# Splitting four weight tiles of the second layer during the first layer's FFN

## The chip, the cores and the metric

The kernel runs on one core of a Trainium2 chip. The metric is the device time of one execution in microseconds (us). A chip has several engines with a queue each: TensorE (PE) multiplies, VectorE (DVE), ScalarE (ACT) and GpSimd (POOL) work element by element, and SyncE (SP) issues the transfers from memory. Each engine takes its instructions strictly in the order of its own list.

## The reference

A two-layer decoder trunk on 512 tokens of width 1024. What matters here is the seam between layer 0's feed-forward part and layer 1's attention:

```
x = x + (jax.nn.silu(g) * u) @ ffn_w_down[i]            # end of layer 0
h = rmsnorm(x, attn_norm[1])
cols = split_cols(h @ nsa_w_in[0], NSA_COLS)             # q, kc, vc, ks, vs, kw, vw, gates
k_cmp = gelu(blocks(kc + pos) @ ck_w1) @ ck_w2           # compression of keys
v_cmp = gelu(blocks(vc + pos) @ cv_w1) @ cv_w2           # compression of values
o = g0 * attend(q, k_cmp, v_cmp) + g1 * attend(rope(q), rope(ks), vs) + g2 * attend(rope(q), rope(kw), vw)
```

Layer 1 has 12 query heads in 6 pairs and three branches of attention: over compressed blocks, over selected blocks (keys `ks`), and over a window (keys `kw`).

## The kernel before, in words

**Products in two parts.** Every weight tile is 128 x 1024 and is multiplied in a split form: `hi` is the tile rounded to a shorter float, `lo` is what is missing, and a product is three matmuls, hi x hi, hi x lo of the activations, and lo x hi (lines 177, 178 and 179 of `mm3`). A projection of one 128-column tile is 8 x 3 = 24 matmuls of 512 columns.

**Splitting a weight.** `weight` (line 159) takes the next place of three rings, loads the raw tile (SP, line 163), makes `hi` by a cast (ACT at line 150 or DVE at line 148) and `lo` by a subtraction (DVE at line 165, or POOL, which goes through `Pieces` at line 83 in pieces of 256 columns, four to a tile). Which engine does it is read from the strings of `PLAN`, one after the other. The rings have 4 raw places, 3 for `hi` and 3 for `lo`, so that a tile can be split only when PE has finished the tile three before it.

**The FFN.** `ffn` (line 594) goes through two halves of 11 blocks. For each block two tiles (`g` and `u`, 22 loads `in_wf` in a half) are multiplied with x, then ACT, POOL and DVE make silu(g) * u (lines 606 to 609) and split it (lines 611 and 612); the 11 split blocks are `acts`. After that, 8 output tiles are made from `acts` with two weight tiles each (`in_wd`, 768 and 640 columns). In the second half of layer 0 each output tile also gives the next layer's input `xh`, `xl` and a square for the norm.

**The start of layer 1.** `nsa` (line 897) runs the words of `SEQ[1]`: `vc ks kc q:0 v ck kw h:0 plan:5 cv q:1 c:0 ...`. `vc`, `kc`, `ks`, `kw` and `q:j` are projections of one tile. `v` is `values` (line 970), 96 matmuls of 292 columns into four banks of PSUM, which ACT and DVE then empty (lines 989, 990, 991). `ck` and `cv` are `compress` (line 862) for keys and values: `cy` tiles are made by DVE (line 874), cast by ACT (875) and split by POOL; then come 16 steps of two matmuls, of 128 and 64 columns (lines 880, 881), half of them with the weight tile `cw1[which, 0]` and half with `cw1[which, 1]`; a gelu (lines 883 to 893) and one more product (line 944) follow. `h`, `w` and `c` are a head's scores in the three branches (lines 380 and 381, 385, 391, 409 to 411), capital letters the products with the values behind them (transposes at line 418, copies at 426 and 427, products at 441).

**What sets the order.** The words are only the order in which the program is written. The build gives every instruction a place in its engine's list by a model of its own, so that the four lists interleave several words, and a small change moves instructions further down too.

**The tag `xg`.** `BUFS` has 8 places of 128 x 1024 under the tag `xg`. Before the change only the end of layer 1 uses them (`last_gain`, line 633, and `down_last`, line 639).

Of the kernel before, what the change touches and what calls it, by code (L numbers as in the profile page):

```python
# [11 lines left out]
F32R = mybir.dt.float32r  # L12
# [6 lines left out]
P = 128  # L19
S = 512  # L20
# [9 lines left out]
OUT = -3e38  # L30
DOWN_SPLIT = (6, 5)
HALVED = 2
LAST = ("PPVP", "VVVV")
BUFS = {"xs": 17, "p": 10, "u": 8, "q": 12, "z": 2, "q1": 8, "qi": 4, "cy": 2, "k": 8, "m": 6, "r": 3, "t": 6, "o": 26, "o2": 6, "xg": 8}
RINGS = {"wr": 4, "wh": 3, "wl": 3}
# [29 lines left out]
W1 = ["kc", "vc", "ks", "kw"] + [f"q{j}" for j in range(6)] + ["qm0", "qm1"]  # L65


def r32(ap):
    return ap.bitcast(F32)
# [25 lines left out]
class Trunk:  # L95
# [498 lines left out]
    def ffn(self, i):  # L594
        nc, io = self.nc, self.io
        xs, row = self.xs, None
        for half in range(2):
            acts = []
            for e in range(NFF // 2):
                j = half * (NFF // 2) + e  # L600
                g = self.proj(io["wf"][i, 2 * j], xs)
                u = self.proj(io["wf"][i, 2 * j + 1], xs, "S")
                if row is None:
                    row = self.stats()[1]
                a = self.slot("t", "fa")
                nc.vector.tensor_mul(a, g, row)  # L606
                nc.scalar.activation(a, a, AF.Silu)  # L607
                self.pool.tensor_mul(a, a, row)
                nc.vector.tensor_mul(a, a, u)  # L609
                hi, lo = self.pair("o", "f")  # L610
                nc.scalar.copy(hi, a)
                nc.vector.tensor_sub(lo, a, r32(hi))
                acts.append((hi, lo))
            for d in range(KC):
                if i and half and d == KC - HALVED:
                    self.down_last(acts)
                    break
                ps = self.ps("mm")
                k = 0
                for m in DOWN_SPLIT:  # L620
                    w = self.weight(io["wd"][i, half, d, :, k * P : (k + m) * P], m * P)
                    for e in range(m):
                        sl = slice(e * P, (e + 1) * P)
                        self.mm3(ps, (w[0][:, sl], w[1][:, sl]), acts[k], k == 0, k == NFF // 2 - 1)
                        k += 1
                nc.vector.tensor_add(self.x[d], self.x[d], ps)  # L626
                if half:
                    self.absorb(d, 1 if i == 0 else None)
                    if i:
                        self.last_gain(d, slice(0, S))  # L630


    def last_gain(self, c, sl):
# [5 lines left out]
    def down_last(self, acts):  # L639

        nc, cs, ws = self.nc, range(KC - HALVED, KC), []
        for c in cs:
# [14 lines left out]
        for h in range(2):  # L657
# [11 lines left out]
            flat = self.slot("r", "row")[:, :NM]  # L669
            for m in sorted(range(KC // 2), key=lambda m: LAST[h][m], reverse=True):  # L670
                o = self.slot("p", "out").rearrange("p (e t) -> p e t", e=2)
                wide = lambda t: t[:, None, :].to_broadcast([P, 2, NM])
                if LAST[h][m] == "V":
                    nc.vector.tensor_mul(o, self.xg[m][:, :, sl], wide(row))
                else:
                    if LAST[h].index("P") == m:
                        nc.scalar.copy(flat, row)
# [184 lines left out]
    def compress(self, z, which):  # L862

        nc, io = self.nc, self.io
        pos = self.small(16, "pos", bufs=2)
        nc.sync.dma_start(pos, io["pos"][which])
        ps = self.ps("mm")[:, :P]
        split = lambda t: t.rearrange("p (g c j) -> p g c j", g=2, j=8)
        for u in range(2):
            full = self.slot("t", "cy")  # L870
            both = self.slot("cy", "cy", F32R, 2 * S).rearrange("p (a n) -> p a n", a=2)
            nc.gpsimd.memset(split(full)[:, :, 31], 0.0)
            for g in range(2):
                nc.vector.tensor_add(split(full)[:, g, :31], split(z)[:, g, u : u + 31], pos[:, None, 8 * u : 8 * u + 8].to_broadcast([P, 31, 8]))
            nc.scalar.copy(both[:, 0], full)
            self.pool.tensor_sub(both[:, 1], full, r32(both[:, 0]))
            hi, lo = self.weight(io["cw1"][which, u], 8 * P)
            for j in range(8):
                js = slice(j * P, (j + 1) * P)
                nc.tensor.matmul(ps, hi[:, js], both[:, :, j::8], start=u + j == 0, stop=False)  # L880
                nc.tensor.matmul(ps[:, :64], lo[:, js], both[:, 0, j::8], start=False, stop=u == 1 and j == 7)
        hid = self.small(64, "gh", bufs=2)
        nc.scalar.copy(hid, ps[:, :64])
        nc.vector.tensor_add(hid, hid, ps[:, 64:])
        t = self.small(64, "gt", bufs=2)
        o = self.small(128, "go", bufs=1)
        nc.scalar.activation(t, hid, AF.Square)
        nc.vector.tensor_scalar(t, t, 0.044715, 1.0, op0=ALU.mult, op1=ALU.add)
        nc.vector.tensor_mul(t, t, hid)
        nc.scalar.activation(t, t, AF.Tanh, scale=float(np.sqrt(2 / np.pi)))  # L890
        ov = o.rearrange("p (g e c) -> p g e c", g=2, e=2)
        for e in range(2):
            nc.vector.scalar_tensor_tensor(ov[:, :, e], t.rearrange("p (g c) -> p g c", g=2), 1.0, hid.rearrange("p (g c) -> p g c", g=2),
                                           op0=ALU.add, op1=ALU.mult)
        return ov

    def nsa(self):
        nc, io = self.nc, self.io
        xs = self.xs
        w = {n: io["w1"][t] for t, n in enumerate(W1)}  # L900
        lay = self.lay
        self.cmask, self.cm01 = (lay[:, n * P : (n + 1) * P].rearrange("p (b c) -> p b c", b=NB) for n in range(2))
        cw2, self.gates = lay[:, 2 * P : 2 * P + 192], lay[:, 2 * P + 192 :].rearrange("p (b h) -> p b h", b=NB)
        for t, n in ((self.cmask, "cmask"), (self.cm01, "cm01"), (cw2, "cw2")):
            nc.sync.dma_start(t, io[n])

        col, row = self.stats()
        self.plan(4)
        self.o, self.ready, q = {}, {"row"}, {}
        self.turn = self.flip = False  # L910

        def query(j):
            ps = self.proj(w[f"q{j}"], xs)
            self.o[j] = self.parts(self.rowed(ps, row), self.pair("o", "o"))
            q[2 * j], q[2 * j + 1] = self.stacks(self.rope(ps, tabs), "q1")

        mkv, z, keys = [], {}, {}
        tabs = self.tables(row)

        def key(n):  # L920
            keys[n == "kw"] = self.twins(self.rope(self.proj(w[n], xs), tabs))

        def unfold(n):
            z[n] = self.unfold(self.proj(w[n], xs), row)

        def comp_keys():
            self.comp_keys(self.compress(z["kc"], 0), cw2)

        def comp_values():
            self.comp_values(self.compress(z["vc"], 1), cw2)  # L930

        heads = [self.nsa_units(h, q, keys) for h in range(NH)]
        does = {"q": query, "mq": lambda j: self.mem_query(j, w, xs, row), "ks": lambda: key("ks"), "kw": lambda: key("kw"), "kc": lambda: unfold("kc"),
                "vc": lambda: unfold("vc"), "ck": comp_keys, "cv": comp_values, "v": lambda: self.values(col, xs),
                "mkv": lambda: mkv.extend(self.mem_kv(1)), "o": lambda n: self.out_part(1, n % KC, CHUNKS[1][n // KC], "mm"), "plan": self.plan}
        units = {"c": self.comp_unit, "h": lambda h: heads[h][0], "w": lambda h: heads[h][1],
                 "m": lambda j: self.mem_unit(j, mkv)}
        self.pipeline(SEQ[1], units, does)
        self.add_out(1)
# [228 lines left out]
```

## Time and profile before

| what | value |
|---|---|
| time, median of 3 runs | 1274.98 us (1273.6 to 1275.56) |
| time of the profiled execution | 1277.64 us |
| its span, first to last instruction | 1275.9 us |
| PE busy | 1234.9 us, 97% |
| DVE / ACT / POOL busy | 622.1 / 545.7 / 798.4 us |
| mean granted clock of PE | 0.98 |

The profiled execution took 2.66 us more than the median of the runs. A row of the profile gives a start or a window in us from the first instruction. Busy PE time is modelled from overlapping matmuls, so that a busy PE may still be slow; the granted clock (1.00 is 2.4 GHz, 0.50 is 1.2 GHz) stands beside it. In square brackets at the end of an instruction's row stands how long its engine had idled before it, and which instruction ended that.

### The profile page before, as it was taken

To read this page: it belongs to the slowest core of one execution; us is meant where nothing else is said; L and a number is where in the kernel's file an instruction comes from. 1 tells how busy PE (TensorE), PEld (TensorE's weight loads), DVE (VectorE), ACT (ScalarE), POOL (GpSimd) and SP (SyncE) were. 2 spreads that over 40 slices of the span, in tenths; PEclk is the share of its full clock that TensorE was granted. 3 is DMA by queue.
4 is the path that set the end of the run, shared out by engine and by line. 5 is a ranking of instruction groups with operands and counts; after the bars stand their busy time and mean duration, and the time that the engine had idled before them with its cause. 6 is when DMAs were issued, how large, how long until landed. Compare 5 with 4: busy or idle time off the path is not lost.

```text
span 1275.9 us, 17100 instructions
## 1 busy us (share of the span) xinstructions
PE 1234.9 (97%) x5882; PEld 1026.0 (80%) x5882; DVE 622.1 (49%) x1379; ACT 545.7 (43%) x1059; POOL 798.4 (63%) x1124
## 2 busy tenths in 40 slices
PE   7999889999999999999999999999999999999996
PEld 5888558888888888888888788887888888888886
DVE  6799976632221222234678998896521210111113
ACT  5535896433321223332247776785333322322231
POOL 9988884865543455447277674355986645667573
PEclk9999999999999999999986999999999999999998
DMA  7222002333223333223321101103232234333231
GB/s 267 89 74 89 11 1 76 99 99 99 89 78 100 118 95 99 81 89 116 107 99 50 36 15 57 32 32 118 78 96 96 85 88 114 111 97 91 69 91 66
DMA packets 40262, 108.44 MB, mean 85 GB/s; under 512 B 4720, under 2 KB 10480, under 8 KB 40176
## 3 DMA queue, kind: packets, MB, share of 16 engines
q1 hardware_dynamic: 40176, 107.36, 27.2%
q8 instruction: 46, 0.75, 0.3%
q14 instruction: 40, 0.33, 0.1%
HBM read 105.25 MB, written 2.10 MB: 84 GB/s over the span
## 4 chain that ended last, share of the span: by engine, by line
PE 77%; DVE 14%; ACT 3%; POOL 2%; DMA 2%; issue 1%; SPq 0%; DVEq 0%; ACTq 0%; POOLq 0%
PE ps L179 23%; PE ps L178 23%; PE ps L177 23%; PE ps L441 3%; PE ps L418 2%; DVE sc L690 2%; DVE stay L689 2%; DVE p L385 1%; DVE ul L427 1%; DMA mem<-in_memT 1%; POOL sq L83 1%; PE ps L380 1%; ACT p L391 1%; PE ps L381 1%; POOL stay L83 1%
## 5 line engine op out<-in xcount | busy, mean ns | idle before, releaser
L83 POOL TENSOR_TENSOR stay<-stay,stay 128x256 fp32r<-128x256 f32 (+1 forms) x601 | 441.5, 764 | 306.7 <-ACT stay L150 166.0
L150 ACT CAST stay<-stay 128x1024 fp32r<-128x1024 f32 (+4 forms) x208 | 189.4, 911 | 518.6 <-PE ps L178 455.3
L177 PE MATMUL ps<-xh,stay 128*128 128x512 f32 x912 | 358.9, 394 | 6.8 <-ACT xh L238 6.5
L179 PE MATMUL ps<-xh,stay 128*128 128x512 f32 x912 | 359.1, 394 | 1.2 <-DVE stay L165 1.2
L178 PE MATMUL ps<-xl,stay 128*128 128x512 f32 x912 | 358.0, 393 | 0.5 <-DVE xl L239 0.5
L177 PEld LDWEIGHTS ps<-xh,stay 128*128 128x128 f32 x912 | 173.4, 190 | 43.1 <-ACT xh L238 6.5
L179 PEld LDWEIGHTS ps<-xh,stay 128*128 128x128 f32 x912 | 173.0, 190 | 37.6 <-DVE stay L165 1.5
L178 PEld LDWEIGHTS ps<-xl,stay 128*128 128x128 f32 x912 | 172.9, 190 | 37.0 <-DVE xl L239 1.0
L178 PE MATMUL ps<-fl,stay 128*128 128x512 f32 (+1 forms) x352 | 134.8, 383 | 0.0
L179 PE MATMUL ps<-fh,stay 128*128 128x512 f32 (+1 forms) x352 | 134.6, 382 | 0.0
L177 PE MATMUL ps<-fh,stay 128*128 128x512 f32 (+1 forms) x352 | 134.6, 382 | 0.0
L609 DVE TENSOR_TENSOR fa<-fa,ps 128x512 f32<-128x512 f32 x44 | 30.2, 687 | 183.5 <-PE ps L179 166.1
L626 DVE TENSOR_TENSOR stay<-stay,ps 128x512 f32<-128x512 f32 x30 | 20.7, 689 | 155.6 <-PE ps L179 155.6
L606 DVE TENSOR_TENSOR fa<-ps,row 128x512 f32<-128x512 f32 x44 | 30.2, 690 | 128.2 <-PE ps L179 116.5
L391 ACT ACTIVATE p<-p,stay 128x384 f32<-128x384 f32 (+3 forms) x144 | 80.2, 559 | 18.0 <-DVE stay L385 17.4
L83 POOL TENSOR_TENSOR fa<-fa,row 128x256 f32<-128x256 f32 x88 | 65.3, 764 | 24.9 <-ACT fa L607 24.9
L177 PEld LDWEIGHTS ps<-fh,stay 128*128 128x128 f32 x352 | 66.1, 188 | 12.9
L178 PEld LDWEIGHTS ps<-fl,stay 128*128 128x128 f32 x352 | 66.1, 188 | 12.9
L179 PEld LDWEIGHTS ps<-fh,stay 128*128 128x128 f32 x352 | 66.2, 188 | 12.8
L83 POOL TENSOR_TENSOR p<-p,stay 128x128 f32<-128x128 f32 (+1 forms) x106 | 56.1, 557 | 32.4 <-DVE stay L401 21.7
L427 DVE TENSOR_TENSOR ul<-ps,uh 128x512 fp32r<-128x512 f32 (+1 forms) x103 | 62.7, 619 | 7.1 <-ACT uh L426 5.3
L418 PE MATMUL ps<-stay,p 128*128 128x128 f32 x360 | 55.8, 278 | 5.1 <-POOL p L83 2.1
(273 smaller groups left out, 2018.2 us busy)
## 6 DMA issues: line engine op xcount, KB each, us to landing
stay<-in_wf SPq DMA_DIRECT2D x88, 512.0 KB, 3.6
stay<-in_w SPq DMA_DIRECT2D x26, 512.0 KB, 3.5
stay<-in_wd SPq DMA_DIRECT2D x32, 384.0 KB, 3.1
stay<-in_wd SPq DMA_DIRECT2D x32, 320.0 KB, 2.9
mem<-in_memT SPq DMA_DIRECT2D x12, 256.0 KB, 3.8
stay<-in_wo SPq DMA_DIRECT2D x6, 512.0 KB, 3.5
stay<-in_wo SPq DMA_DIRECT2D x16, 192.0 KB, 2.4
stay<-in_xT SPq DMA_DIRECT2D x8, 256.0 KB, 6.7
```

Of the source, the lines that this page charges most:

```text
L83: op(out[:, sl], x[:, sl], y[:, sl])
L150: self.nc.scalar.copy(out, x)
L177: mm(out, lhs[0], rhs[0], start=start, stop=False)
L178: mm(out, lhs[0], rhs[1], start=False, stop=False)
L179: mm(out, lhs[1], rhs[0], start=False, stop=stop)
L391: self.nc.scalar.activation(p, p, AF.Exp, scale=-1.0, bias=least, accum_out=total)
L418: nc.tensor.transpose(ps[:, off : off + P], ap, self.ident)
L427: nc.vector.tensor_sub(lo, ps[:, :w], r32(hi))
L441: self.nc.tensor.matmul(out, v if len(parts) > 1 else r32(v), t, start=start and i == 0, stop=stop and i == len(parts) - 1)
L606: nc.vector.tensor_mul(a, g, row)
L609: nc.vector.tensor_mul(a, a, u)
L689: nc.vector.max(m8, s)
```

## The change

`split_early` is called once, in the second half of layer 0's FFN, between the 22 `wf` tiles and the 16 `wd` tiles. For each of four tiles of layer 1 (both tiles of the compression of keys, the projection of `kw`, and the second pair's queries) it takes a raw place of the ring, loads it, casts it on ACT into a place of the tag `xg`, and subtracts on POOL into another. It takes no places of the `hi` and `lo` rings and no letters of `PLAN`. `compress` and `nsa` use the split tiles where they exist; `proj` (line 181) already accepts a split tile. So in the window from `ck` to `q:1` four calls of `weight` fall away: by the letters of plans 4 and 5 these were two casts on ACT and one on DVE with two subtractions on DVE and one on POOL for `cw1[0, 0]`, `cw1[0, 1]` and `kw`, and a cast on ACT with a subtraction on POOL for `q:1`.

```diff
--- before.py
+++ after.py
@@ -30,6 +30,7 @@
 OUT = -3e38
 DOWN_SPLIT = (6, 5)
 HALVED = 2
+EARLY = ("cw00", "cw01", "kw", "q1")
 LAST = ("PPVP", "VVVV")
 BUFS = {"xs": 17, "p": 10, "u": 8, "q": 12, "z": 2, "q1": 8, "qi": 4, "cy": 2, "k": 8, "m": 6, "r": 3, "t": 6, "o": 26, "o2": 6, "xg": 8}
 RINGS = {"wr": 4, "wh": 3, "wl": 3}
@@ -611,6 +612,8 @@
                 nc.scalar.copy(hi, a)
                 nc.vector.tensor_sub(lo, a, r32(hi))
                 acts.append((hi, lo))
+            if i == 0 and half == 1:
+                self.split_early()
             for d in range(KC):
                 if i and half and d == KC - HALVED:
                     self.down_last(acts)
@@ -628,6 +631,16 @@
                     self.absorb(d, 1 if i == 0 else None)
                     if i:
                         self.last_gain(d, slice(0, S))
+
+    def split_early(self):
+
+        nc, self.early_w = self.nc, {}
+        for n in EARLY:
+            raw, hi, lo = next(self.rings["wr"]), self.slot("xg", "wx", F32R, 2 * S), self.slot("xg", "wx", F32R, 2 * S)
+            nc.sync.dma_start(raw, self.io["w1"][W1.index(n)] if n in W1 else self.io["cw1"][int(n[2]), int(n[3])])
+            nc.scalar.copy(hi, raw)
+            self.pool.tensor_sub(lo, raw, r32(hi))
+            self.early_w[n] = hi, lo
 
 
     def last_gain(self, c, sl):
@@ -874,7 +887,7 @@
                 nc.vector.tensor_add(split(full)[:, g, :31], split(z)[:, g, u : u + 31], pos[:, None, 8 * u : 8 * u + 8].to_broadcast([P, 31, 8]))
             nc.scalar.copy(both[:, 0], full)
             self.pool.tensor_sub(both[:, 1], full, r32(both[:, 0]))
-            hi, lo = self.weight(io["cw1"][which, u], 8 * P)
+            hi, lo = self.early_w.get(f"cw{which}{u}") or self.weight(io["cw1"][which, u], 8 * P)
             for j in range(8):
                 js = slice(j * P, (j + 1) * P)
                 nc.tensor.matmul(ps, hi[:, js], both[:, :, j::8], start=u + j == 0, stop=False)
@@ -897,7 +910,7 @@
     def nsa(self):
         nc, io = self.nc, self.io
         xs = self.xs
-        w = {n: io["w1"][t] for t, n in enumerate(W1)}
+        w = {n: io["w1"][t] for t, n in enumerate(W1)} | self.early_w
         lay = self.lay
         self.cmask, self.cm01 = (lay[:, n * P : (n + 1) * P].rearrange("p (b c) -> p b c", b=NB) for n in range(2))
         cw2, self.gates = lay[:, 2 * P : 2 * P + 192], lay[:, 2 * P + 192 :].rearrange("p (b h) -> p b h", b=NB)
```

The lists of three engines change as follows (lines below 614 of the changed file are one higher than before, those of `compress` and after it 13 higher).

PE, right after the values: the compression of keys (`cy`, lines 880 and 881, in the changed file 893 and 894) and the projection of `kw` (`xh`, `xl`). Before:

```order
L177 MATMUL ps_5180<-xh_4409,stay_65 128x512
L178 MATMUL ps_5180<-xl_4410,stay_65 128x512
L881 MATMUL ps_5104<-cy_5133,stay_65 128x64
L880 MATMUL ps_5104<-cy_5133,stay_65 128x128
L881 MATMUL ps_5104<-cy_5133,stay_65 128x64
L880 MATMUL ps_5104<-cy_5133,stay_65 128x128
L380 MATMUL ps_5233<-th_4881,sa_4970 128x256
L381 MATMUL ps_5233<-tl_4882,sa_4970 128x256
L881 MATMUL ps_5104<-cy_5133,stay_65 128x64
L880 MATMUL ps_5104<-cy_5133,stay_65 128x128
L881 MATMUL ps_5104<-cy_5133,stay_65 128x64
L179 MATMUL ps_5180<-xh_4409,stay_65 128x512
```

In the changed program:

```order
L893 MATMUL ps_5136<-cy_5162,wx_4374 128x128
L894 MATMUL ps_5136<-cy_5162,wx_4375 128x64
L178 MATMUL ps_5200<-xh_4441,wx_4382 128x512
L179 MATMUL ps_5200<-xl_4442,wx_4382 128x512
L180 MATMUL ps_5200<-xh_4441,wx_4383 128x512
```

Before, the second half of the compression is interleaved with `kw` and with two scores of the first head. Now all 32 matmuls of the compression stand in one piece, all 24 of `kw` in the next, and both read the tiles `wx` of the early split; the two scores follow behind.

ACT, while the values' banks are emptied and the keys' compression begins. Before:

```order
L150 CAST stay_65<-stay_64 128x1024
L991 ACT_TABLE_LOAD
L991 ACTIVATE stay_64<-ps_4978,stay_64 128x36
L989 ACTIVATE stay_65<-ps_4979,stay_64 128x4x64
L989 ACTIVATE stay_65<-ps_4980,stay_64 128x4x64
L989 ACTIVATE stay_65<-ps_4981,stay_64 128x4x64
L991 ACTIVATE stay_64<-ps_4979,stay_64 128x36
L150 CAST stay_65<-stay_64 128x1024
L991 ACTIVATE stay_64<-ps_4980,stay_64 128x36
L991 ACTIVATE stay_64<-ps_4981,stay_64 128x36
L150 CAST stay_65<-stay_64 128x1024 x2
L883 COPY stay_64<-ps_5104 128x64
```

In the changed program:

```order
L151 CAST stay_65<-stay_64 128x1024
L1004 ACT_TABLE_LOAD
L1004 ACTIVATE stay_64<-ps_5010,stay_64 128x36
L151 CAST stay_65<-stay_64 128x1024
L1002 ACTIVATE stay_65<-ps_5011,stay_64 128x4x64
L1002 ACTIVATE stay_65<-ps_5012,stay_64 128x4x64
L1004 ACTIVATE stay_64<-ps_5011,stay_64 128x36
L1002 ACTIVATE stay_65<-ps_5013,stay_64 128x4x64
L151 CAST stay_65<-stay_64 128x1024
L1004 ACTIVATE stay_64<-ps_5012,stay_64 128x36
L1004 ACTIVATE stay_64<-ps_5013,stay_64 128x36
L896 COPY stay_64<-ps_5136 128x64
```

The cast ahead of the table load was that of the first compression tile and is now that of a tile of the values' compression; the list has three casts before line 883 (now 896) instead of four, and one of them now stands ahead of the emptying of the second and third bank. That third cast is the next query tile's: it stood further on, ahead of the second half of the `kw` keys (line 366), and has moved up to here.

POOL, at the end of the `wf` tiles and the begin of the `wd` tiles in layer 0 (`fa` is the multiplication inside silu(g) * u, `stay` the splits of the rings). Before:

```order
L83 TENSOR_TENSOR stay_65<-stay_64,stay_65 128x256 x8
L83 TENSOR_TENSOR fa_4215<-fa_4215,row_2528 128x256 x2
L83 TENSOR_TENSOR stay_65<-stay_64,stay_65 128x256 x4
L83 TENSOR_TENSOR fa_4287<-fa_4287,row_2528 128x256 x2
L83 TENSOR_TENSOR stay_65<-stay_64,stay_65 128x256 x3
L83 TENSOR_TENSOR fa_4356<-fa_4356,row_2528 128x256 x2
L83 TENSOR_TENSOR stay_65<-stay_64,stay_65 128x256 x5
L83 TENSOR_TENSOR stay_65<-stay_64,stay_65 128x128
```

In the changed program:

```order
L84 TENSOR_TENSOR stay_65<-stay_64,stay_65 128x256 x8
L84 TENSOR_TENSOR fa_4215<-fa_4215,row_2528 128x256 x2
L84 TENSOR_TENSOR wx_4367<-stay_64,wx_4366 128x256 x4
L84 TENSOR_TENSOR wx_4375<-stay_64,wx_4374 128x256 x4
L84 TENSOR_TENSOR stay_65<-stay_64,stay_65 128x256 x4
L84 TENSOR_TENSOR wx_4383<-stay_64,wx_4382 128x256 x4
L84 TENSOR_TENSOR fa_4287<-fa_4287,row_2528 128x256 x2
L84 TENSOR_TENSOR stay_65<-stay_64,stay_65 128x256 x3
L84 TENSOR_TENSOR wx_4391<-stay_64,wx_4390 128x256 x4
L84 TENSOR_TENSOR fa_4356<-fa_4356,row_2528 128x256 x2
L84 TENSOR_TENSOR stay_65<-stay_64,stay_65 128x256 x5
L84 TENSOR_TENSOR stay_65<-stay_64,stay_65 128x128
```

Sixteen pieces `wx` come in between: two tiles ahead of the last `wf` split, one behind it and ahead of a block's `fa`, one ahead of the last block's `fa`. In SP's list the loads of the two compression tiles stand ahead of the first `wd` load, that of `kw` behind the first and that of `q:1` behind the second.

## Rows read from the trace of the kernel before

**Rows 1.** The page: busy time of each engine, and the granted clock in 40 slices.

```profile
PE 1234.9 (97%) x5882; PEld 1026.0 (80%) x5882; DVE 622.1 (49%) x1379; ACT 545.7 (43%) x1059; POOL 798.4 (63%) x1124
...
PEclk9999999999999999999986999999999999999998
```

**Rows 2.** Windows: us, busy PE, PEld, DVE, ACT, POOL, granted clock, DMA share, GB/s.

```profile
500.00:560.00 60.00, 60.00 (x266) 49.68 (x265) 16.94 (x22) 17.84 (x23) 28.54 (x39) 1.00 0.26 78
...
645.00:651.00 6.00, 5.38 (x37) 4.41 (x36) 5.48 (x8) 5.14 (x10) 5.92 (x6) 1.00 0.24 90
651.00:658.00 7.00, 6.51 (x21) 5.54 (x21) 2.84 (x6) 1.67 (x4) 6.73 (x12) 0.51 0.64 224
...
664.00:672.00 8.00, 8.00 (x56) 7.34 (x54) 7.40 (x20) 6.60 (x17) 4.17 (x6) 0.98 0.20 67
672.00:692.00 20.00, 17.64 (x67) 15.46 (x67) 15.11 (x41) 13.16 (x33) 17.91 (x25) 0.50 0.24 80
692.00:740.00 48.00, 45.00 (x269) 38.91 (x268) 46.43 (x136) 37.23 (x100) 33.27 (x50) 1.00 0.11 34
```

**Rows 3.** The chain that ended last, 600 to 720 us: start, us, what.

```profile
645.66 2.23 POOL cy L83 x2
...
648.35 3.10 POOL stay L83 x3
651.50 0.42 PE ps L881
...
672.04 1.03 ACT stay L150
```

**Rows 4.** PE in order of time: start, us, instruction, idle before it.

```profile
646.16 0.27 PE L880 MATMUL ps<-cy,stay 128*128 128x128 f32 x1
646.72 0.30 PE L881 MATMUL ps<-cy,stay 128*128 128x64 f32 x1 [0.29 <-DVE stay L165]
...
651.50 0.42 PE L881 MATMUL ps<-cy,stay 128*128 128x64 f32 x1 [0.49 <-POOL stay L83]
...
653.44 0.77 PE L179 MATMUL ps<-xh,stay 128*128 128x512 f32 x1
...
660.02 0.39 PE L177 MATMUL ps<-xh,stay 128*128 128x512 f32 x1
660.25 0.39 PE L178 MATMUL ps<-xl,stay 128*128 128x512 f32 x1
...
660.70 0.33 PE L944 MATMUL ps<-stay 128*128 128x64 f32 x2
...
667.74 0.27 PE L880 MATMUL ps<-cy,stay 128*128 128x128 f32 x1
...
671.46 0.28 PE L179 MATMUL ps<-stay,ol 128*128 128x64 f32 x1
```

**Rows 5.** Windows of 1 us, columns as in rows 2: where the clock changes.

```profile
651.00:652.00 1.00, 0.51 (x4) 0.51 (x3) 0.53 (x1) 0.00 (x0) 1.00 (x2) 0.59 0.00 0
...
658.00:659.00 1.00, 1.00 (x6) 0.82 (x5) 0.00 (x0) 0.00 (x0) 0.00 (x0) 0.99 0.60 57
...
671.00:672.00 1.00, 1.00 (x10) 1.00 (x9) 1.00 (x2) 1.00 (x3) 0.00 (x0) 0.83 0.00 0
...
692.00:693.00 1.00, 1.00 (x6) 0.80 (x5) 1.00 (x6) 0.87 (x4) 0.32 (x1) 0.93 0.00 0
```

**Rows 6.** ACT, POOL and DVE in order of time, 645 to 675 us.

```profile
646.23 0.29 ACT L991 ACTIVATE stay<-ps,stay 128x36 f32<-128x36 f32 x1
...
645.66 2.74 POOL L83 TENSOR_TENSOR cy<-cy,cy 128x256 fp32r<-128x256 f32 x2
...
673.74 1.24 DVE L367 TENSOR_TENSOR tl<-ra,th 64x512 fp32r<-64x512 f32 x1 [0.81 <-ACT th L366]
```

**Rows 7.** POOL and PE in order of time, end of layer 0's second half.

```profile
534.23 2.82 POOL L83 TENSOR_TENSOR stay<-stay,stay 128x256 fp32r<-128x256 f32 x4 [6.67 <-issue]
537.01 1.44 POOL L83 TENSOR_TENSOR fa<-fa,row 128x256 f32<-128x256 f32 x2
538.39 2.14 POOL L83 TENSOR_TENSOR stay<-stay,stay 128x256 fp32r<-128x256 f32 x3
545.67 1.43 POOL L83 TENSOR_TENSOR fa<-fa,row 128x256 f32<-128x256 f32 x2 [5.14 <-ACT fa L607]
...
549.35 0.39 PE L177 MATMUL ps<-fh,stay 128*128 128x512 f32 x1
```

**Rows 8.** The page's DMA issues: KB each, median us from issue to landing.

```profile
stay<-in_w SPq DMA_DIRECT2D x26, 512.0 KB, 3.5
```

## The prediction

> **What bounds the kernel now.** I read the page first: TensorE is busy 97% of the span and its granted clock is full but for a dent just past the middle [rows 1]. That dent is the first half of layer 1's attention, and the windows open it up: at 651 to 658 us the clock stands at 0.51, at 672 to 692 at 0.50, and beside them TensorE is not even busy all the time, 5.38 of 6 us, 6.51 of 7 and 17.64 of 20 [rows 2]. From 692 us VectorE takes over: 46.43 of 48 us busy. So this stretch has three limits in a row: weights that are split late, a halved clock (1.2 in place of 2.4 GHz), and then VectorE.
>
> The chain of waits says what is late. From 645.66 it runs through POOL, first the second `cy` tile of the keys' compression and then three pieces of a weight split (3.10 us), and only then to the compression's matmuls at 651.50 [rows 3]. The matmuls in order of time show the same: the compression stands at 646.72 for a split by VectorE, at 651.50 for one by POOL, and is through at 653.44, when `kw` at last runs without a break; `kw` ends at 660.70 [rows 4]. In the changed program these splits are done during the FFN, so I rework this stretch.
>
> **Part 1, the compression of keys.** It still cannot start before its bank of PSUM is emptied: the gates' activation starts at 646.23 and takes 0.29, so 646.52 [rows 6], and on ACT the same amount stands ahead of it as before. What 32 such matmuls cost with everything there is shown by the compression of values: 667.74 to 671.46, 3.72 us, 1.86 for 16 [rows 4]. The first 16 run to 648.38. The second 16 need the second `cy` tile, which POOL finishes at 645.66 + 2.74 = 648.40 [rows 6]; the change leaves that alone. They end at 648.40 + 1.86 = 650.26. What is late next is thus POOL's `cy`, no longer a weight.
>
> **Part 2, `kw`.** 24 matmuls at full clock follow each other by 0.23 us (660.02, 660.25) [rows 4]: 5.52 us, so an end at 655.78. The open price is the clock. Before, it fell at 651.2 and came back at 658.0 [rows 5], 4.6 us after `kw` began to run unbroken at 653.44. The 3.7 us of the values' compression, without a wait, were also followed by a fall, at 671.7 [rows 4, 5], though TensorE was busy 8.00 of 8 us [rows 2]. So I let the clock fall here too, at 651.2, and come back 4.6 us after 650.26, at 654.9: 3.7 us at half clock lose 1.85. `kw` ends at 657.63 and the lead is 660.70 - 657.63 = **3.07 us**. The ends: with no fall 4.92; with a fall as long as before (6.8 us, 3.4 lost) 1.52. I take the middle value since it keeps the return that the rows show.
>
> The Trainium skill speaks for the better end: TensorE: Matmul & The Clock Gate, section "Why this matters for your kernels", ties a drop of throughput in mid-kernel to idle gaps of TensorE between bursts of matmuls. By that rule there would be no fall in the changed program and the lead would be 4.9. The trace does not bear this out alone: the fall at 671.7 has no idle gap before it.
>
> **Part 3, a cast less in the chain.** At 672.04 ACT casts the next query tile, 1.03 us in the chain of waits [rows 3], and VectorE stands 0.81 us for the key casts queued behind it [rows 6]. In the changed list this cast stands earlier, before the gelu. I count **0.81**, between 0 (something else is late) and 1.03.
>
> **Part 4, edits that I cost at nothing.** VectorE loses three instructions near 645 to 651; it idles right afterwards (2.84 of 7 us busy [rows 2]), so their end gains nothing but what part 1 has. `q:1` comes ready, but of the 7.0 us from 660.70 to 667.74 [rows 4] its own matmuls take 5.5 and the scores among them the rest, so nothing is gained there beyond the lead. One cast now stands ahead of the emptying of the second and third bank, 1.03 us [rows 3]; the bank that `kw` takes is emptied behind 646.52 by two casts (2.06) and five short activations (some 0.29 each, as the one in rows 6, 1.5), at about 650.1, just before the compression ends; so it is hidden, barely. The four loads leave a window with a DMA share of 0.64 for one with 0.26 [rows 2].
>
> In the FFN, POOL gets 16 pieces of 2.82 / 4 = 0.705 us, 11.3 us, and ACT four casts, 4.1 us. POOL was busy 28.54 of 60 us and ACT 17.84 [rows 2], and between 527 and 549 POOL alone has gaps of 6.67 and 5.14 us [rows 7]. The first `wd` split, 538.39 to 540.53, moves behind four pieces and a delayed `fa`, to about 543.4; TensorE wants it at 549.35 [rows 7]. These 6 us are the cover. If they were used up, every late piece would stop TensorE for its own length.
>
> **The sum.** 3.07 + 0.81 = 3.9 us, with ends of 1.5 and 5.9. The profiled execution itself took 1277.64 us and would come to 1273.7; it stands 2.66 above the median of the runs, 1274.98, and against that the forecast is **1271.1 us**. It asks that the lead lasts to the end. For that speaks that VectorE's list after 692 us starts with the data of this stretch and is no longer than before, so that a start 3.9 us sooner shifts it whole.
>
> **The rivals.** A change of 0.2%, 2.55 us, is about what a measurement of this kernel tells from none, and the bound for the chances.
>
> *No fall of the clock during `kw`.* The 24 dense matmuls come 3.2 us sooner and close the slow stretch before the clock falls. Lead 4.9 + 0.8 = 5.7: 1269.3 us. (The rule of the Trainium skill cited in part 2 gives this case.) For it: the slow stretch shrinks from 7.3 us (646.16 to 653.44) to 3.8. Against it: 671.7. Chance 0.15.
>
> *The lead is halved in the second dent.* The clock was half until 692.1 [rows 5]. If it comes back at that time however early the work stands there, the last us before run at half clock and half of 3.9 is lost: gain 1.95, 1273.0 us. The same time comes out if VectorE, 97% busy afterwards, has the lead taken by other work. Chance 0.27.
>
> *Slower: the new lists of the attention stall TensorE and the clock falls once more.* The order of scores, transposes and products is not the same after 692 us. TensorE idles 3.0 of 48 us there, at full clock [rows 2]. If the new order doubles that, 3.0, and the clock falls for twice as long as at 651.2, 13.6 us, 6.8 are lost by it: 3.0 + 6.8 - 3.9 = 5.9 slower, 1280.9 us. It decides as soon as the granted clock between 692 and 740 leaves 1.00. For it: the clock has fallen twice shortly before. Against: VectorE's work is the same, and those 3.0 us of idle time did not move the clock. Chance 0.10.
>
> *Slower: the FFN loses its cover.* The load of `kw` stands behind the first `wd` load, and its cast and its pieces stand ahead of a block's silu and `fa`. A load takes 3.5 us to land [rows 8]; three one after the other, 10.5, use up the 6 and stop TensorE for 4.5, and a fall of the clock as at 651.2 adds 3.4: 7.9 - 3.9 = 4.0 slower, 1279.0 us. Against it: the raw ring has four places and the tiles are loaded well ahead. Chance 0.05.
>
> That the change does not do what it says is excluded: the lists show the tiles `wx` in the compression, in `kw` and in `q:1`.
>
> **How the numbers follow.** My forecast has 0.43. Of it 0.08 lie under 2.55 us, by its lower end of 1.5. Faster: 0.35 + 0.15 + a quarter of the halved case, 0.07, is 0.57. Same: 0.08 + 0.20 = 0.28. Slower: 0.15. The range goes from 1267.5 (no fall, and the better half of the runs' spread of 2 us) to 1276.5 (the lead gone and 1.5 lost by the new order); outside lie the most of the two slower cases, 0.13, and about 0.05 below.
>
> **What would show it.** Right in part 1: no wait for a weight split in the compression's matmuls, its 32 in one piece of about 3.7 us, `kw` starting within 0.3 us of its end. Part 2: from the first compression matmul to the end of `kw` 11.1 us in place of 14.5, with 3 to 4 us at half clock. Part 3: VectorE no longer waits for the key casts. Part 4: TensorE without a gap between 540 and 600 us. It would be wrong if the stretch from 645 us to the first `wf` matmul of layer 1 does not shorten by the lead at `kw`'s end, or if POOL's 16 pieces show up as idle time of TensorE in the FFN.

## The result, and the profile after

The changed kernel took **1267.65 us** (median of 7 runs, 1263.59 to 1270.73) against 1275.11 for the kernel before in the same session (7 runs, 1273.6 to 1276.11). The ratio is 0.9938, with a 95% interval from 0.9928 to 0.9948: 7.5 us faster. Two repeats of the same file gave 1265.11 and 1267.14; the median of all its 15 runs is 1266.63. The forecast was 1271.1, a gain of 3.9. The sign was right, but the gain is about twice the sum. That the median lies inside the range, which began at 1267.5, is luck: the ratio, put on the 1274.98 from which the forecast started, gives 1267.1, and the median of all 15 runs lies below the range as well.

The page of the profiled execution, which with 1263.59 us was the quickest of its seven:

```profile
PE 1222.8 (97%) x5882; PEld 1015.3 (80%) x5882; DVE 621.3 (49%) x1376; ACT 545.8 (43%) x1060; POOL 803.0 (64%) x1132
...
PEclk9999999999999999999998999999999999999998
```

Against [rows 1] TensorE issues the same 5882 matmuls and is busy 12.1 us less. The dent of the clock past the middle, 8 and 6 before, is a single 8. The windows over the stretch (columns as in rows 2):

```profile
500.00:560.00 60.00, 60.00 (x266) 49.67 (x265) 20.56 (x21) 20.83 (x26) 40.97 (x56) 1.00 0.38 117
...
645.00:651.00 6.00, 6.00 (x34) 5.15 (x33) 3.12 (x8) 2.53 (x8) 6.00 (x10) 1.00 0.43 107
651.00:658.00 7.00, 7.00 (x36) 5.96 (x35) 5.93 (x20) 4.20 (x13) 3.89 (x8) 1.00 0.38 134
664.00:672.00 8.00, 6.58 (x32) 5.52 (x31) 5.44 (x14) 4.82 (x13) 8.00 (x13) 0.74 0.23 68
672.00:692.00 20.00, 19.16 (x97) 16.45 (x97) 18.43 (x72) 15.11 (x48) 13.22 (x21) 0.85 0.18 51
692.00:740.00 48.00, 45.18 (x270) 38.85 (x270) 46.12 (x124) 35.64 (x90) 35.07 (x51) 1.00 0.09 24
```

Between 651 and 658 us the clock is full where it was 0.51 [rows 2], and between 672 and 692 it is 0.85 where it was 0.50. POOL's 16 added pieces show in the first line, 40.97 us against 28.54, and TensorE is busy for all 60 us of it, as before. After 692 VectorE is the bound as before.

TensorE in order of time (start, us, instruction, idle before it):

```profile
642.63 0.27 PE L893 MATMUL ps<-cy,wx 128*128 128x128 f32 x1
642.72 0.24 PE L894 MATMUL ps<-cy,wx 128*128 128x64 f32 x1
...
646.05 0.24 PE L894 MATMUL ps<-cy,wx 128*128 128x64 f32 x1
646.12 0.48 PE L178 MATMUL ps<-xh,wx 128*128 128x512 f32 x1
...
651.45 0.39 PE L180 MATMUL ps<-xh,wx 128*128 128x512 f32 x1
651.68 0.28 PE L381 MATMUL ps<-th,sa 128*128 128x256 f32 x1
```

No row carries an idle time, where [rows 4] had waits for VectorE and POOL. The compression is one piece of 3.49 us (642.63 to 646.12), and the 24 matmuls of `kw` take 5.56 us (646.12 to 651.68).

Starts cannot be compared directly, since earlier stretches of two executions differ by a few us (the values' first matmul stands at 633.34 us before and at 629.81 after). So the table counts from that matmul. Its last columns are a third profile of the changed kernel, of an execution of 1267.73 us, close to the median (the values start there at 630.80). Each lead is what is left when the time after is taken from the time before.

| us after the values' first matmul | before | after | lead | third profile | lead |
|---|---|---|---|---|---|
| first matmul of the keys' compression | 12.82 | 12.82 | 0 | 12.82 | 0 |
| last matmul of `kw` done | 27.36 | 21.87 | 5.49 | 21.87 | 5.49 |
| first matmul of the values' compression | 34.40 | 28.81 | 5.59 | 28.81 | 5.59 |
| its last matmul | 38.05 | 32.24 | 5.81 | 32.24 | 5.81 |
| first matmul of `q:2` | 58.47 | 48.56 | 9.91 | 48.71 | 9.76 |
| first matmul of `q:4` | 87.36 | 79.29 | 8.06 | 80.88 | 6.48 |
| first sum of squares for layer 1's FFN | 282.00 | 271.51 | 10.49 | 274.64 | 7.35 |
| end | 642.52 | 632.00 | 10.51 | 635.15 | 7.37 |

The third profile ends with a lead of 7.37 us, close to the measured gain of 7.5. The quicker execution has 3 us more because the clock did not fall at two places where it did in the third: at 700.0 us (3.4 us long) and at 880.9 us (3.4 us; before has one at 890.1). The account below therefore uses the third profile.

### The profile page after: what moved, and what is told of

Same layout as the page of the kernel before. It is cut to its first block, busy times and chain, and to the rows that moved or that the text cites. A ratio compares the mean times of both kernels' runs of the same rounds, so it can differ in the third digit from the quotient of the medians.

```text
span 1261.8 us, 17118 instructions
## 1 busy us (share of the span) xinstructions
PE 1222.8 (97%) x5882; PEld 1015.3 (80%) x5882; DVE 621.3 (49%) x1376; ACT 545.8 (43%) x1060; POOL 803.0 (64%) x1132
## 4 chain that ended last, share of the span: by engine, by line
PE 81%; DVE 11%; POOL 3%; ACT 2%; issue 1%; DMA 0%; SPq 0%; DVEq 0%; ACTq 0%; POOLq 0%
PE ps L179 23%; PE ps L180 23%; PE ps L178 23%; PE ps L442 4%; PE ps L419 2%; POOL sq L84 2%; DVE sc L703 2%; DVE stay L702 2%; DVE p L386 1%; PE ps L381 1%; PE ps L382 1%; DVE ul L428 1%; ACT p L392 1%; PE ssq L202 1%; POOL stay L84 1%
## 5 line engine op out<-in xcount | busy, mean ns | idle before, releaser
L84 POOL TENSOR_TENSOR stay<-stay,stay 128x256 fp32r<-128x256 f32 (+1 forms) x593 | 433.4, 760 | 288.6 <-ACT stay L151 132.0
L151 ACT CAST stay<-stay 128x1024 fp32r<-128x1024 f32 (+5 forms) x205 | 186.2, 908 | 496.8 <-PE ps L179 429.6
L178 PE MATMUL ps<-xh,stay 128*128 128x512 f32 x896 | 350.3, 391 | 6.3 <-ACT xh L239 6.3
L180 PE MATMUL ps<-xh,stay 128*128 128x512 f32 x896 | 350.7, 392 | 1.2 <-DVE stay L166 1.2
L179 PE MATMUL ps<-xl,stay 128*128 128x512 f32 x896 | 350.0, 391 | 1.2 <-DVE xl L240 1.2
L178 PEld LDWEIGHTS ps<-xh,stay 128*128 128x128 f32 x896 | 168.7, 188 | 41.5 <-ACT xh L239 6.8
L179 PEld LDWEIGHTS ps<-xl,stay 128*128 128x128 f32 x896 | 168.6, 188 | 36.9 <-DVE xl L240 2.3
L180 PEld LDWEIGHTS ps<-xh,stay 128*128 128x128 f32 x896 | 168.7, 188 | 36.1 <-DVE stay L166 1.5
L166 DVE TENSOR_TENSOR stay<-stay,stay 128x1024 fp32r<-128x1024 f32 (+4 forms) x36 | 45.3, 1259 | 25.6 <-ACT stay L151 24.9
```

The source lines that it names most:

```text
L84: op(out[:, sl], x[:, sl], y[:, sl])
L151: self.nc.scalar.copy(out, x)
L166: self.engine("w").tensor_sub(lo, raw, r32(hi))
L178: mm(out, lhs[0], rhs[0], start=start, stop=False)
L179: mm(out, lhs[0], rhs[1], start=False, stop=False)
L180: mm(out, lhs[1], rhs[0], start=False, stop=stop)
```

## The experiments

Two theories stood after the result. The first (A in the first expectations): the clock explains it, and with the time lost to the half clock taken out both kernels need the same. The rival: the work itself got shorter, because weights no longer come late, and the clock follows from that. A third question was whether the FFN pays. `EARLY` names the tiles split early: `cw00` and `cw01` are the keys' compression, `cw10` and `cw11` the values'.

**The early splits are made but not used.** Layer 1 splits its own tiles as before.

```diff
-            hi, lo = self.early_w.get(f"cw{which}{u}") or self.weight(io["cw1"][which, u], 8 * P)
+            hi, lo = self.weight(io["cw1"][which, u], 8 * P)
...
-        w = {n: io["w1"][t] for t, n in enumerate(W1)} | self.early_w
+        w = {n: io["w1"][t] for t, n in enumerate(W1)}
```

> The four tiles are loaded and split in layer 0's FFN as in the change, but nobody uses them: layer 1 splits its own again, so that its lists are those of the kernel before. This prices the added work of the FFN alone (16 POOL pieces, four casts, four loads). Theory A (the gain is mostly TensorE's clock) and theory B (the gain is the removed waits) both expect no change: 1275 us, within 2.5. If the FFN's cover were used up, it would be over 2.5 us slower and TensorE would show gaps between 540 and 600 us.

It took 1276.36 us (10 runs) against 1275.81, ratio 1.0004, interval 0.9994 to 1.0013. Its windows:

```profile
500.00:560.00 60.00, 60.00 (x267) 49.67 (x266) 17.19 (x21) 21.00 (x26) 42.57 (x57) 1.00 0.39 117
560.00:600.00 40.00, 40.00 (x178) 33.14 (x177) 14.00 (x16) 12.44 (x17) 27.00 (x35) 1.00 0.35 103
```

TensorE has no gap in 100 us although POOL carries the 16 pieces. No price of the FFN is seen (the interval reaches 0.0013, or 1.7 us), and nothing of the gain comes from there.

**The keys' compression alone, and its complement.**

```diff
-EARLY = ("cw00", "cw01", "kw", "q1")
+EARLY = ("cw00", "cw01")
```

> Only the two tiles of the compression of keys are split early; kw and q:1 are split in layer 1 as before. Theory B, by removed waits: the compression is through at about 650.3 in place of 653.4, a gain of about 3 us of the 7.5, so 1272. Theory A, by the clock (time less what the half clock takes is the same in both kernels, about 1250 us): without kw ready the slow stretch is not closed, the clock still falls as often as before, and the gain is under 2 us, 1273.5 or more, with a mean clock of 0.980 to 0.982.

```diff
-EARLY = ("cw00", "cw01", "kw", "q1")
+EARLY = ("kw", "q1")
```

> Only kw and q:1 are split early; the two tiles of the compression are split in layer 1 as before, so that the compression still waits for its weights. Theory B: POOL and VectorE are relieved of kw and q:1, kw runs at once after the compression; a gain of 3 to 4 us, 1271 to 1272. Theory A: what counts is whether TensorE is kept busy densely enough after the values; with the waits of the compression still there the clock falls at about 651 as before, gain 2 to 3 us, mean clock about 0.982.

The compression's tiles alone gave 1269.24 us (4 runs), ratio 0.9953 (0.9938 to 0.9968), 6.6 us less than the 1275.81 of the kernel before in that session and better than either theory had it. The complement gave 1270.83 (10 runs), 0.997 (0.9959 to 0.9981), 5.0 us less. In the same session the whole change took 1265.11 us (next experiment), ratio 0.9924, 10.7 us less. So the parts add up to the change within the intervals: 11.6 against 10.7 us by the medians, 0.77% against 0.76% by the ratios.

They do their work at different places. In the first, `kw` is split late as before and still ends 22.02 us after the values' start, a lead of 5.34 against the change's 5.49; two tiles fewer stand ahead of it on the engines that split. So `kw`'s own early split adds about 0.15 us at that place. In the complement (its profile is of an execution of 1273.59 us, 2.8 above its median) `kw` ends at 23.50, a lead of 3.86, and the lead at the values' compression is 3.90. Behind that compression lies the second dent, the half clock from 671.7 to 692.1 us in the kernel before. There the complement gains 3.46 more (`q:2` at 51.11 against 58.47, lead 7.36), and its dent is 6.8 us long (from 671.3); the compression's tiles alone gain nothing there.

In the complement the clock also fell during `kw`, at 654.2 us for 3.4 us. Its windows, and its TensorE there:

```profile
645.00:651.00 6.00, 6.00 (x40) 5.52 (x39) 5.70 (x8) 5.34 (x10) 5.84 (x7) 1.00 0.26 69
651.00:658.00 7.00, 7.00 (x40) 6.14 (x40) 2.67 (x6) 3.34 (x8) 7.00 (x11) 0.76 0.47 136
```

```profile
650.60 0.22 PE L894 MATMUL ps<-cy,stay 128*128 128x64 f32 x1
...
653.91 0.24 PE L894 MATMUL ps<-cy,stay 128*128 128x64 f32 x1
653.97 0.57 PE L180 MATMUL ps<-xh,wx 128*128 128x512 f32 x1
```

The wait for the compression's late weights is filled here by eleven of `kw`'s matmuls, which are ready; TensorE does not idle, all but the first of the compression's matmuls stand in one piece, and the clock falls at their end all the same.

The kernel with the compression's tiles alone shows such a fall too, behind the values' compression. Windows of 1 us:

```profile
663.00:664.00 1.00, 1.00 (x11) 1.00 (x10) 0.97 (x2) 1.00 (x3) 0.00 (x0) 1.00 0.00 0
664.00:665.00 1.00, 1.00 (x8) 1.00 (x6) 1.00 (x4) 0.95 (x3) 0.00 (x0) 0.54 0.00 0
```

and its TensorE there:

```profile
663.94 0.34 PE L893 MATMUL ps<-cy,stay 128*128 128x128 f32 x1
664.10 0.33 PE L894 MATMUL ps<-cy,stay 128*128 128x64 f32 x1
664.24 0.40 PE L180 MATMUL ps<-stay,ol 128*128 128x64 f32 x1
```

The clock stood at half for 20.5 us from 664.1, as long as before from 671.7. In that kernel the lead at the end of the values' compression is 5.33 and at `q:2` 5.39: the second dent gave it nothing.

**The changed kernel again.**

> The changed kernel once more, for the spread of its runs and the clock of each. Theory A: in every run the span less (1 - mean clock) x span is 1250 to 1252 us, as in the profile of the kernel before (1275.9 at 0.980: 1250.4) and of the changed one (1261.8 at 0.992: 1251.7), so that times from 1263 to 1271 go with clocks from 0.992 to 0.985. Theory B: the times differ from the kernel before by a fixed lead of about 7 us, and this difference less the clock's part is clearly above 2 us.

It took 1265.11 us (4 runs, 1263.62 to 1266.63), ratio 0.9924 (0.9907 to 0.994). With all runs at hand the first theory can be tried at equal clock. At a mean granted clock of 0.988 the kernel before took 1273.0 to 1275.2, the changed one 1266.47 to 1267.65. So 7 us remain where the clock's mean is the same: the theory that with the clock taken out both need the same falls. In the changed kernel the spread between runs goes with the clock (0.992 with 1263.6, 0.985 with 1267.9 to 1270.7), but the difference of the kernels does not. In the kernel before even the spread hardly does: over the sessions of these experiments its 14 runs at 0.981 have a median of 1276.1, its 8 runs at 0.987 one of 1275.5. This is the mean over a whole execution; what a fall in this one stretch costs is tried further below.

**Two other pairs beside the compression's tiles.** Are `kw` and `q:1` special?

```diff
-EARLY = ("cw00", "cw01", "kw", "q1")
+EARLY = ("cw00", "cw01", "q1", "q2")
```

> The early tiles are those of the compression of keys, q:1 and q:2; kw is split in layer 1 as before. The engines' lists are otherwise those of the changed kernel. Theory A: kw's early split is not needed (with the compression's tiles alone kw already ended 5.1 us sooner than before), and what counts besides is how much split work POOL and ACT still have when the attention starts; as good as the change or better, 1264 to 1268. Theory B: kw must be ready at the end of the compression; without it 2 to 3 us of the change's gain are lost, 1269 to 1271.

```diff
-EARLY = ("cw00", "cw01", "kw", "q1")
+EARLY = ("cw00", "cw01", "cw10", "cw11")
```

> The early tiles are both tiles of the compression of keys and both of that of values; kw and q:1 are split in layer 1. Theory A: any four tiles less relieve POOL and ACT by the same amount, 1265 to 1268. Theory B: q:1 and kw are what the first scores wait for; no better than with the two tiles of the keys alone, 1269.

They took 1268.32 us (0.9945, 0.9929 to 0.9962) and 1266.77 (0.9935, 0.9921 to 0.995), 4 runs each. The second is as good as the change; the first lies between its two theories, and its interval holds both the change's ratio and that of the compression's tiles alone (0.9953). The second dent was 13.7 us long in the one and 10.2 in the other. So `kw` and `q:1` are not needed for the gain, since the values' tiles do as well; whether any pair would do is not shown, as the pairs differ by 1.5 us, about as far as the intervals reach.

**Matmuls nobody reads, to hold the clock.** If the clock's dent behind the values' compression costs time, matmuls laid into the wait there should give it back; if the waits alone set the pace, they should give nothing. The word `f:12` stands in `SEQ[1]` between `w:0` and `c:1`, first in the changed kernel, then in the kernel before:

```diff
+        def fill(n):
+            ps, k = self.ps("T", "fill"), keys[True][0][0]
+            for i in range(n):
+                nc.tensor.matmul(ps, k[:, :P], xs[i % KC][0], start=i == 0, stop=i == n - 1)
```

> The changed kernel with 12 more matmuls of 512 columns (2.7 us at full clock), whose result nobody reads, right before the first head's transposes, where TensorE waits and the clock falls at 668 us for 10.2 us. Theory A, the halved clock is what costs there: the clock stays at full, up to 5 us come back for 2.7 us of added work, 1263 to 1266. Theory B, the stretch is bound by the chain through ACT, POOL and VectorE and the clock only follows: no gain, 1267 to 1270, whether the clock falls or not.

> The kernel before with the same 12 idle matmuls in the same place, where the clock is half for 20.5 us from 671.7 on. Theory A: if the clock stays at full, up to 10 us come back for 2.7 us of added work, 1268 to 1272. Theory B: no gain, 1275 to 1278.

In the changed kernel 1264.02 us (4 runs, 1263.4 to 1264.98), ratio 0.9915 (0.9901 to 0.993); in the kernel before 1272.71 (10 runs), 0.9983 (0.9973 to 0.9992). Windows of the filled changed kernel:

```profile
664.00:672.00 8.00, 7.39 (x51) 6.54 (x51) 6.71 (x16) 6.06 (x16) 8.00 (x12) 1.00 0.20 68
672.00:692.00 20.00, 18.86 (x109) 15.64 (x109) 19.68 (x79) 16.41 (x52) 14.72 (x24) 1.00 0.19 53
```

The clock is full in both windows; in this execution it fell later, at 696.4 us, for 3.4 us. The same window of the filled kernel before, [rows 2] without:

```profile
672.00:692.00 20.00, 18.80 (x98) 15.81 (x97) 18.10 (x55) 15.47 (x43) 18.33 (x27) 0.90 0.25 79
```

There the half clock shrank from 20.5 to 6.8 us and the lead at `q:2` was 3.77. Without any change to the weights, 2.9 us come back with the filling, a time between the ranges of the two theories.

Is it the clock that gives them back? In the changed kernel the gain goes with it: all eight runs with 6 (below) or 12 idle matmuls have a mean clock of 0.991 to 0.994 and took 1262.94 to 1264.98 us; of the 15 runs without filling three have 0.991 or 0.992, and these took 1263.59 to 1264.24, no more. The filling makes the good execution the usual one. In the kernel before it is not shown: at 0.987 and 0.988, on the same chip, the filled kernel has a median of 1272.67 (7 runs) and the unfilled one of 1275.33 (7 runs), so that 2.7 us remain at equal mean clock. There the order of the lists, which the filling changes too, is a rival that no run excludes.

**How much filling.** The same with 6 and with 24, with the third profile of the changed kernel beside them, and the filling of 12 with the other pair of tiles.

> The changed kernel with 6 idle matmuls in place of 12 (1.4 us). Theory A: they fill half of the wait; the clock falls in some executions and not in others, 1264 to 1267, with a wider spread than with 12. Theory B (order of the lists): the lists behind differ from those with 12, so the time may land anywhere from 1263 to 1270 whatever the clock does between 664 and 690.

> The changed kernel with 24 idle matmuls (5.4 us), more than the wait holds. Theory A: the clock stays full as with 12, but some 2 to 3 us of the fill now stand in the way of the first head's transposes: 1265 to 1268. Theory B: as for 6.

> The changed kernel again, beside the three others on the same chip. Both theories: 1264 to 1268, clocks from 0.985 to 0.992, and a fall of the clock near 668 us for 7 to 14 us, none while kw runs.

> Early tiles: both of the compression of keys and both of that of values, and the 12 idle matmuls before the first head's transposes. Theory A (the clock's second fall is a cost of its own, on top of the split work): the two add up, the clock stays full from 664 to 690, 1262 to 1264, under the kernels with either alone (1266.8 and 1264.0). Theory B (the fill's gain was a lucky order of the lists behind it): no better than 1266.

Six gave 1263.82 us (4 runs, 1262.94 to 1264.96), ratio 0.99 (0.9886 to 0.9915), the lowest median of all; 24 gave 1266.23 (0.991, 0.9887 to 0.9934), with a fall of 3.4 us at 692.6 us in its profile; the changed kernel on that chip 1267.14 (0.9925, 0.9911 to 0.994). With six:

```profile
664.00:672.00 8.00, 7.02 (x48) 5.83 (x47) 6.76 (x19) 5.91 (x17) 8.00 (x12) 1.00 0.20 68
672.00:692.00 20.00, 17.70 (x101) 14.32 (x100) 19.83 (x76) 15.87 (x51) 13.55 (x23) 1.00 0.16 52
692.00:740.00 48.00, 44.63 (x259) 38.16 (x258) 44.45 (x117) 33.43 (x83) 33.90 (x50) 1.00 0.08 23
```

and on TensorE, in order of time:

```profile
663.54 1.54 PE L948 MATMUL fill<-xh,th 128*128 128x512 f32 x6
```

Six matmuls take 1.54 us and were enough in that execution. Its lead is 13.55 us at `q:2`, 10.80 at `q:4` and 10.52 at the end. With the clock full, VectorE is busy 19.83 of 20 us, and nearly 3 us of the lead are given back; at the end it is no larger than that of the quicker execution without filling (10.51). The filling of 12 with the values' tiles split early did not add up: 1266.54 us (0.9923, 0.9902 to 0.9944), no better than without it (1266.77), as the theory of a lucky order had it, and the clock fell all the same, at 671.4 us for 6.8. The lists behind the filling differ in each of these four kernels, so the number of matmuls is not the only thing changed between them, and the runs don't say which part of a difference is which.

## Why the prediction was right or wrong

**Part 1, the compression: right in kind, 0.6 us too small.** There is no wait for a weight split and the 32 matmuls stand in one piece. Two waits that I put in their place did not come. I let the first matmul wait until 646.52 us for a bank of PSUM; yet it follows the values' last matmul at once, 12.82 us after their start, before and after. [rows 4] showed it at 646.16, 0.36 us sooner. And POOL's second `cy` tile, "late next", was ready in time. POOL after the change (start, us, instruction):

```profile
642.22 1.42 POOL L84 TENSOR_TENSOR cy<-cy,cy 128x256 fp32r<-128x256 f32 x2
643.61 8.36 POOL L84 TENSOR_TENSOR stay<-stay,stay 128x256 fp32r<-128x256 f32 x12
```

Its two pieces took 1.42 us where they had taken 2.74 [rows 6]. They end at 643.64, and the second 16 matmuls begin at 644.33. With 2.74 they would have ended at 644.96 and cost a wait of 0.6. The prediction costed VectorE's three lost instructions at nothing; the neighbour that they had slowed is the item missing there.

**Part 2, `kw`: this is the step that failed.** "So I let the clock fall here too, at 651.2, and come back 4.6 us after 650.26, at 654.9: 3.7 us at half clock lose 1.85." It did not fall. `kw` ended 21.87 us after the values' start where I had 24.29 (657.63 less 633.34): 0.6 of the difference is Part 1, 1.8 the clock. The lead there is 5.49, not 3.07, and lies above even the end that I called "no fall", 4.92. It is not one execution only. In all ten profiles of kernels with the compression's tiles split early no fall stands between the compression and 664 us; in all four without (before, the unused splits, the complement, the filled kernel before) one stands between 648.8 and 654.2, of 6.8 us in three and 3.4 in the complement. So the fall goes away with the late splits of the compression's weights. Why it does is open: idle waits were not needed for it, since in the complement TensorE had none and the clock fell. The rival "no fall during `kw`", to which I gave 0.15, was the case for this step; its whole gain, 5.7, was nearer than mine, but the rest came from terms behind `kw` that no case had. The rule of the Trainium skill (TensorE: Matmul & The Clock Gate, section "Why this matters for your kernels") speaks of idle gaps between bursts. The traces agree only in part: the changed kernel has no gap there and no fall, but the waits before were of 0.29 and 0.49 us [rows 4], shorter than the gaps that the page names. I had held the fall at 671.7 us against the rule, and that fall remains outside it, as do those at 654.2 in the complement and at 664.1 with the compression's tiles alone, each with TensorE busy ahead of it.

**Part 3, a cast less: the wait is gone, its size not seen by itself.** The casts and subtractions of the keys now follow each other without VectorE idling, at 661.78 us and 662.48, so the 0.81 [rows 6] is gone. But before, it stood in the second dent (673.74 us), across which the lead grows from 5.81 to 9.8, and no run separates the two.

**Part 4, costed at nothing: right.** No price of the FFN is seen (unused splits, ratio 1.0004), so that the rival of the lost cover falls. Between `kw` and the values' compression the lead moved from 5.49 to 5.59, as I had said of `q:1`.

**The second dent, taken as unchanged: wrong, and the other way than its rival.** I let the lead pass it whole and gave 0.27 to its being halved. It grew instead. TensorE of the changed kernel, in order of time:

```profile
666.60 0.22 PE L442 MATMUL ps<-uh,stay 128*128 128x128 f32 x1
667.89 0.47 PE L442 MATMUL ps<-ul,stay 128*128 128x128 f32 x1 [1.08 <-DVE ul L428]
```

and windows of 1 us, where the clock falls and returns:

```profile
668.00:669.00 1.00, 1.00 (x4) 1.00 (x5) 1.00 (x3) 0.44 (x1) 1.00 (x2) 0.50 0.20 37
...
678.00:679.00 1.00, 1.00 (x6) 0.83 (x6) 1.00 (x5) 0.35 (x1) 0.00 (x0) 0.95 0.00 0
```

The clock falls later, in a wait for VectorE's `ul`, and stands at half for 10.2 us (667.9 to 678.1) instead of 20.5 [rows 5]. The lead gains 3.95 us from the values' compression to `q:2` (third profile, 5.81 to 9.76). After that the VectorE-bound stretch takes 3.28 back by `q:4`. Of this some 1.4 to 1.7 are a clock fall of that execution: half of its 3.4 us at 700 us are 1.7, and the quicker execution, without it, gives back 1.85, which is 1.43 less. Windows of the third profile:

```profile
692.00:740.00 48.00, 44.87 (x261) 38.64 (x260) 44.63 (x122) 36.14 (x92) 35.00 (x50) 0.96 0.08 28
...
700.00:704.00 4.00, 4.00 (x15) 3.56 (x15) 3.94 (x10) 1.21 (x2) 1.33 (x2) 0.58 0.00 0
```

**The sum as it came out:** 5.49 at `kw`, 0.32 to the end of the values' compression, 3.95 in the second dent, 3.28 given back, 0.89 on the way to the end: 7.37 us. Against the 3.9 of the forecast, 2.4 are missing at `kw` and about 1 behind it. The slower rival of a third fall had its mechanism (the fall at 700 us) but a fall of 3.4 us could not outweigh the rest.

**What stays open.** Why the clock did not fall at `kw`, as said. And why the second dent is shorter: splitting the compression's tiles alone does not do it (20.5 us), `kw` and `q:1` alone make it 6.8, and with `kw` and `q:1`, `q:1` and `q:2`, or the values' tiles beside the compression's it is 10.2, 13.7 and 10.2 us. Each of these also reorders the lists of the attention, and no run kept the lists and moved only the splits. Nor is it settled how much of the 3.28 is the new order and how much VectorE's own work.

## What to carry to other kernels

A weight that comes late can cost more than its wait: with the compression's two tiles split early, waits of 1.1 us on TensorE went (0.29 and 0.49 us in [rows 4], 0.33 at 649.14 us), and with them a fall of the clock of 6.8 us, half of which is lost time. Look at the clock behind a late weight, and count the lead with and without the fall as two cases of their own. When work leaves a window, list also whom it had slowed there; the missing 1.3 us on POOL came from a neighbour and not from the tile. And where a clock dent follows a wait that cannot be removed, six matmuls that nobody reads are a cheap trial: here the changed kernel with them has the lowest time, 1263.82 us against 1267.14 on the same chip. Since they also change the lists behind them, only the time tells whether they pay: 24 of them, or 12 with another pair of tiles, gave nothing beyond the intervals.

## What was not expected of the hardware

**POOL and VectorE.** The same 128 x 256 subtraction of POOL took 1.37 us a piece in the kernel before [rows 6], 645.66 to 648.40 us, and 0.71 in the changed one. What stood beside it before, on VectorE (start, us, instruction):

```profile
645.42 1.25 DVE L165 TENSOR_TENSOR stay<-stay,stay 128x1024 fp32r<-128x1024 f32 x1
646.59 1.22 DVE L148 CAST stay<-stay 128x1024 fp32r<-128x1024 f32 x1
```

After the change VectorE has nothing between 642.05 and 644.42 us. The Trainium skill (GPSIMD Engine Reference, section "Specifications") says that POOL shares its way to SBUF, the memory on the chip that holds the tiles, with VectorE and contends with VectorE's instructions that have two inputs there or run in one of its two-port modes. The rows agree for the subtraction, which has two inputs there: the price was a factor of 1.9 while it and a cast ran. Elsewhere in the kernel before, 305 such pieces with nothing on VectorE took 0.72 to 0.75 us.

**The clock fell with TensorE busy.** At 664.1 us in the kernel with the compression's tiles alone, the clock went to 1.2 GHz at the end of the values' compression, 128- and 64-column matmuls without a gap, and stayed there for 20.5 us; yet the same kind of matmuls at the keys' compression, in the same kernel, was followed by full clock. In the complement it is the keys' compression, again without a gap, behind which the clock fell, at 654.2 us. No run here tells what decides.
